# Summing a norm's squares on TensorE, accumulated in PSUM, instead of on GpSimd and VectorE

## The chip, the cores and the metric

The kernel runs on one core of a Trainium2 chip. A core has five engines with queues of their own: TensorE (PE in the profile, its weight loads PEld), VectorE (DVE), ScalarE (ACT), GpSimd (POOL) and SyncE (SP, which here only issues transfers). Matmuls write to PSUM, eight banks per core; VectorE and ScalarE read PSUM, and GpSimd works on SBUF alone in this kernel. The metric is the device time of one execution in microseconds. The time before is the median of three runs.

## What is computed

Two layers of a trunk over 768 tokens (256 context, 512 latent) of width 1024, one sample, all in float32. Each layer has a mixer and a SwiGLU feed-forward (FFN), and ahead of each of the four stands a modulated RMS norm:

```python
def rms_norm(x, gain):
    xf = x.astype(f32)
    y = xf * lax.rsqrt(jnp.mean(xf * xf, axis=-1, keepdims=True) + EPS)
    return (y * gain.astype(f32)).astype(x.dtype)
...
for l in range(DEPTH):
    h = rms_norm(x, norm_mix[l]) * (1.0 + sc_m) + sh_m
    ...                                    # mixer of the layer, added to x
    hf = rms_norm(x, norm_ffn[l]) * (1.0 + sc_f) + sh_f
    x = x + g_f * swiglu(hf, ffn_w_in[l], ffn_w_out[l])
```

The context tokens go the same way with a modulation of their own in layer 0. The norm that changes is the one ahead of layer 1's mixer, whose input is the output of layer 0's FFN.

## The kernel before, in words

Features lie on the partitions: the stream `x` is eight tiles `x[0]` to `x[7]` of 128 features by 768 tokens. Every dense product is done as three matmuls of split operands (`mm3`, L180): weights and activations are each cut into a high part (`whi`, `hhi`) and a rest (`wlo`, `hlo`).

A scheduler at build time orders the instructions of each engine by priority (the order in which the code is written) and by its own model of when operands are ready. What it wrote down is fixed: an engine executes its queue in that order, and an instruction that waits holds up all that stand behind it on the engine. A tile of a pool with so many buffers waits for the release of an older one. In PSUM the pool `gs` has tags A and B with three banks each and C with two; the norms' sums (`sp`) and broadcasts (`rb`) are of tag C.

Layer 0's FFN ends so (`ffn0`, its last group of hidden tiles): for the feature tiles c = 0, 1, 2 the output product is done for all tokens; for c = 3 to 7 it is done token segment by token segment, first the 256 context tokens (segment 0), then tokens 256 to 511 of the tile (segment 1), then 512 to 767 (segment 2). A product of one c and one segment is 12 matmuls (`f<-mid,v`), and VectorE adds it to `x[c]` (L1592). Behind each, the norm of layer 1's mixer (class `Norm`, named `n1m` in the table `NORMS`) takes up what is there:

- `acc(k, i)`: ScalarE squares tile k of segment i into a buffer `sq` of two (L322), and GpSimd adds it to the segment's sum `ssq` (L324), from k = 5 on VectorE does. The first square of a segment is written into `ssq` itself.
- `finish(i)`: a pair of matmuls of `ssq` with a column of ones sums over the partitions, into a PSUM tile `sp` (L335), one column for each 128 tokens. ScalarE scales it to the mean `ms` (L337); a reciprocal root of 128 by 2 numbers follows, its first step on VectorE (L194) and fourteen small steps on GpSimd (L197 to L206); a pair of matmuls with the unit matrix spreads it over the partitions, `rb` (L341). Then VectorE forms `nt` for each k (L344), ScalarE `hhi` (L356) and VectorE `hlo` (L357), the operands of the mixer's first products (`d<-whi,hhi`), which start with segment 1.

The same class serves the norm ahead of layer 0's FFN (`n0f`, three segments, whose end is at 700 to 727 us) and the norm ahead of layer 1's FFN (`n1f`, two segments, at 1551 to 1575 us). There the sums stay as they are.

Of the kernel before, what the change touches and what calls it, by code (L numbers as in the profile page):

```python
# [7 lines left out]
F32 = mybir.dt.float32  # L8
F32R = mybir.dt.float32r
I32 = mybir.dt.int32  # L10
AF = mybir.ActivationFunctionType
# [8 lines left out]
KT = 8  # L20
# [11 lines left out]
RS_SEED = -1.8352575e-20  # L32

ORDER = "vp0 out1 Ad0 Bd1 vp1 Bd2 Bd3 Ad1 Ad2 G2 G0 Ad3 G1 G3".split()
NORMS = dict(n0f=(5, 'G', (7,)), n1m=(5, 'G', (7,)), n1f=(4, 'G', ()))
FILL = dict(out1=2, Ad0=1, vp1=2, Ad2=1, G2=3, Ad3=1, G1=3)

CONST_W = {}
# [88 lines left out]
def build(tc, a, out, dbg=None):  # L127
    nc = tc.nc
    V, G, S, T, DMA = nc.vector, nc.gpsimd, nc.scalar, nc.tensor, nc.sync
    es = ExitStack()  # L130
    with es:
# [10 lines left out]
        def cc(name):  # L142
            o, n = CONST_W[name]
            return cst[:, o:o + n]

        ident, ones = cc("ident"), cc("le")[:, 127:128]
# [156 lines left out]
        class Norm:  # L303
# [11 lines left out]
            def acc(self, k, i):  # L315
                s, sl = self.segs[i]
                n = sl.stop - sl.start
                first = self.ssq[i] is None
                if first:
                    self.ssq[i] = self.tile(f"ssq{i}", n)  # L320
                sq = self.ssq[i] if first else self.tile("sq", 256, 2)
                S.activation(out=sq, in_=self.x[k][:, sl], func=AF.Square)  # L322
                if not first:
                    (V if k >= self.on_v else G).tensor_tensor(out=self.ssq[i], in0=self.ssq[i], in1=sq, op=ALU.add)  # L324

            def finish(self, i):
                s, sl = self.segs[i]
                n = sl.stop - sl.start
                m = n // 128
                if self.h is None:  # L330
                    self.h = new_h()
                hi, lo = self.h
                sp = self.ps.tile([128, 8], F32, name="sp", tag="C")
                for j in range(m):
                    T.matmul(out=sp[:, j:j + 1], lhsT=self.ssq[i][:, 128 * j:128 * j + 128], rhs=ones, start=True, stop=True)  # L335
                ms = self.tile("ms", m)
                S.activation(out=ms, in_=sp[:, 0:m], func=AF.Identity, scale=1.0 / D, bias=epst)  # L337
# [4 lines left out]
                for k in range(KT):  # L342
                    t = self.tile("nt", 256, 4)
                    V.scalar_tensor_tensor(  # L344
                        out=t, in0=self.x[k][:, sl], scalar=self.av[s][:, k:k + 1], in1=rb, op0=ALU.mult, op1=ALU.mult
# [116 lines left out]
        with tc.tile_pool(name="x0", bufs=1) as x0p:  # L462
# [7 lines left out]
            for k in range(KT):  # L470
                sq = ssq if k == 0 else x0p.tile([128, NT], F32, name="sq", tag="sq", bufs=2)
# [4 lines left out]
            for j in range(4):  # L476
# [10 lines left out]
                sp = x0v.tile([128, 6], F32, name="sp", tag="v3")  # L487
# [6 lines left out]
                for i, sl in enumerate((CTX, LAT)):  # L494
                    n = sl.stop - sl.start
# [1478 lines left out]
```

## Time and profile before

| | |
|---|---|
| median of 3 runs | 1938.0 us (1934.97 to 1938.1) |
| the profiled execution, and its span | 1938.09 us, span 1936.3 us |
| TensorE busy | 1794.5 us, 93% of the span |
| VectorE, ScalarE, GpSimd busy | 1257.4, 805.2, 380.5 us |
| sums of squares on GpSimd, in the three norms that use `Norm` (L324) | 30, of 0.73 to 1.55 us |
| the same on VectorE | 26, of 0.42 us |
| squares on ScalarE (L322) | 64, of 0.42 us |

Times below are microseconds from the span's start. In a row of the timeline stand the start, the time that the entry takes, the engine, the line, the operation, output and inputs, and how many instructions were merged; in brackets the idle time of the engine ahead of it and what ended it. A float32 matmul of this kernel that isn't of split operands shows as two weight loads and two matmuls, so that a pair of them (`sp`, `rb`) is "x4".

### The profile page before, as it was taken

To read this page: it belongs to the slowest core of one execution; us is meant where nothing else is said; L and a number is where in the kernel's file an instruction comes from. 1 tells how busy PE (TensorE), PEld (TensorE's weight loads), DVE (VectorE), ACT (ScalarE), POOL (GpSimd) and SP (SyncE) were. 2 spreads that over 40 slices of the span, in tenths; PEclk is the share of its full clock that TensorE was granted. 3 is DMA by queue.
4 is the path that set the end of the run, shared out by engine and by line. 5 is a ranking of instruction groups with operands and counts; after the bars stand their busy time and mean duration, and the time that the engine had idled before them with its cause. 6 is when DMAs were issued, how large, how long until landed. Compare 5 with 4: busy or idle time off the path is not lost.

```text
span 1936.3 us, 30405 instructions
## 1 busy us (share of the span) xinstructions
PE 1794.5 (93%) x11343; PEld 1623.0 (84%) x11343; DVE 1257.4 (65%) x2839; ACT 805.2 (42%) x1773; POOL 380.5 (20%) x436
## 2 busy tenths in 40 slices
PE   4979999788988958999999999899999989999999
PEld 3867889677877857999999999899999778888887
DVE  6566688676767569988877878746666663433333
ACT  3434454446465355232323323455555342222221
POOL 2132214441201052141231322401010020000000
PEclk8989999899999979999999999899999989999999
DMA  7466645656344622424344334212111212323232
GB/s 300 147 192 206 208 128 151 187 158 196 115 122 152 210 83 66 131 98 124 109 138 138 122 122 133 91 45 77 56 62 45 88 45 87 111 78 119 87 105 92
DMA packets 114436, 238.43 MB, mean 123 GB/s; under 512 B 11920, under 2 KB 51088, under 8 KB 113136
## 3 DMA queue, kind: packets, MB, share of 16 engines
q1 hardware_dynamic: 101760, 208.32, 33.8%
q0 software_dynamic: 4064, 14.38, 2.6%
q10 hardware_dynamic: 8464, 13.79, 2.0%
q8 instruction: 90, 1.47, 0.3%
q14 instruction: 58, 0.48, 0.1%
HBM read 203.44 MB, written 32.99 MB: 122 GB/s over the span
## 4 chain that ended last, share of the span: by engine, by line
PE 72%; DVE 6%; DMA 5%; ACT 3%; POOL 2%; issue 2%; SPq 0%; POOLq 0%; ACTq 0%; DVEq 0%
PE f L180 43%; PE d L180 16%; PE o L180 3%; DMA qkd<-ar 1%; PE sc L1779 1%; PE o L1804 1%; PE m L954 1%; PE S L1250 1%; PE t L1278 1%; DMA st<-in_ada_w_dram 1%; PE m L1793 1%; DVE e L1264 0%; PE m L1052 0%; PE m L1750 0%; PE m L1066 0%
## 5 line engine op out<-in xcount | busy, mean ns | idle before, releaser
L166 ACT ACTIVATE whi<-st 128x1024 fp32r<-128x1024 f32 (+6 forms) x191 | 169.6, 889 | 402.7 <-PE f L180 234.3
L167 DVE TENSOR_TENSOR wlo<-st,whi 128x1024 fp32r<-128x1024 f32 (+6 forms) x191 | 195.9, 1027 | 147.7 <-ACT whi L166 145.6
L180 PE MATMUL d<-whi,hhi 128*128 128x256 f32 (+1 forms) x800 | 235.3, 296 | 18.0 <-ACT ar L211 13.6
L180 PE MATMUL d<-wlo,hhi 128*128 128x256 f32 (+1 forms) x800 | 233.2, 292 | 1.3 <-DVE wlo L167 1.3
L180 PE MATMUL d<-whi,hlo 128*128 128x256 f32 (+1 forms) x800 | 232.7, 292 | 0.0
L180 PE MATMUL f<-hlo,whi 128*128 128x512 f32 (+2 forms) x632 | 229.2, 363 | 2.6 <-DVE hlo L400 2.3
L180 PE MATMUL f<-hhi,whi 128*128 128x512 f32 (+2 forms) x632 | 228.5, 363 | 2.6 <-DVE ev L1549 1.3
L180 PE MATMUL f<-hhi,wlo 128*128 128x512 f32 (+2 forms) x632 | 228.2, 362 | 0.3 <-DVE wlo L1520 0.3
L180 PEld LDWEIGHTS d<-whi,hhi 128*128 128x128 f32 x800 | 157.2, 197 | 24.1 <-ACT ar L211 14.9
L180 PEld LDWEIGHTS d<-wlo,hhi 128*128 128x128 f32 x800 | 157.5, 197 | 2.5 <-DVE wlo L167 1.7
L180 PEld LDWEIGHTS d<-whi,hlo 128*128 128x128 f32 x800 | 157.0, 197 | 1.0
L180 PE MATMUL f<-mid,whi 128*128 128x512 f32 (+1 forms) x624 | 151.5, 337 | 0.0
L180 PE MATMUL f<-v,whi 128*128 128x384 f32 x528 | 138.4, 341 | 3.5 <-ACT v L399 2.2
L180 PEld LDWEIGHTS f<-hlo,whi 128*128 128x128 f32 x632 | 119.5, 189 | 16.6 <-DVE hlo L400 2.8
L180 PEld LDWEIGHTS f<-hhi,whi 128*128 128x128 f32 x632 | 119.3, 189 | 16.4 <-ACT hf L383 1.6
L180 PEld LDWEIGHTS f<-hhi,wlo 128*128 128x128 f32 x632 | 119.5, 189 | 13.6 <-DVE wlo L1520 0.5
L180 PEld LDWEIGHTS f<-mid,whi 128*128 128x128 f32 x624 | 106.9, 189 | 12.8
L1477 POOL TENSOR_TENSOR ws<-st 128x512 f32<-128x512 f32 x22 | 33.3, 1511 | 406.0 <-DMA st<-in_wfi_dram 289.9
L180 PE MATMUL d<-hhi,whi 128*128 128x512 f32 (+1 forms) x304 | 107.7, 354 | 2.8 <-ACT cin L211 1.4
L180 PE MATMUL d<-hhi,wlo 128*128 128x512 f32 (+1 forms) x304 | 105.5, 348 | 0.0
L180 PE MATMUL d<-hlo,whi 128*128 128x512 f32 (+1 forms) x304 | 105.4, 347 | 0.0
L180 PE MATMUL f<-mid,wlo 128*128 128x256 f32 (+1 forms) x312 | 102.5, 336 | 0.0
(410 smaller groups left out, 4348.5 us busy)
## 6 DMA issues: line engine op xcount, KB each, us to landing
st<-in_wfi_dram SPq DMA_DIRECT2D x88, 512.0 KB, 3.3
ast<-in_ada_t_dram SPq DMA_DIRECT2D x96, 256.0 KB, 2.9
st<-in_ada_w_dram SPq DMA_DIRECT2D x32, 512.0 KB, 4.0
aw<-in_ada_dram SPq DMA_DIRECT2D x8, 1024.0 KB, 12.5
st<-in_wfo_dram SPq DMA_DIRECT2D x32, 256.0 KB, 2.9
st<-in_w1kv_dram SPq DMA_DIRECT2D x16, 512.0 KB, 3.2
aqT<-qkd SPq DMA_DIRECT2D x48, 128.0 KB, 3.1
st<-in_wfo_dram SPq DMA_DIRECT2D x16, 384.0 KB, 3.0
```

What stands on the lines that cost most here:

```text
L166: S.activation(out=hi, in_=st, func=AF.Copy)
L167: last_lo[:] = [V.tensor_tensor(out=lo, in0=st, in1=hi.bitcast(F32), op=ALU.subtract).ins]
L180: r = T.matmul(out=ps, lhsT=p, rhs=q, start=(c == 0), stop=(c == n - 1))
L954: T.matmul(out=ps[:, i, :], lhsT=lhs[:, c, :], rhs=rhs[:, c, :], start=True, stop=True)
L1250: T.matmul(out=ps[:, o:o + w], lhsT=u.q[:, part, :], rhs=kst[:, m, sl], start=(i == 0), stop=(i == 1))
L1278: T.matmul(out=ov, lhsT=PT[:, i, :], rhs=vt[:, u.kts[i], :], start=(i == 0), stop=(i == u.nk - 1))
L1477: G.tensor_tensor(out=sa[:, 0:512], in0=a21, in1=a22, op=ALU.add)
L1779: T.matmul(out=o, lhsT=lq[:, q], rhs=kv(lk), start=(i == 0), stop=(i == 2))
L1793: T.transpose(out=tp[:, 128 * i:128 * i + 128], in_=E[:, qi, 128 * b:128 * b + 128], identity=ident)
L1804: T.matmul(out=o, lhsT=lv[:, v, :], rhs=p, start=(n == 0 and i == 0), stop=(n == 5 and i == 2))
```

## The change

For the norm `n1m` alone, the sum over feature tiles moves to TensorE: each square, still made on ScalarE, is at once multiplied with the column of ones, and the eight products of a segment accumulate in its two columns of a PSUM tile `sp`, which is now taken from tag C when the segment's first square is there and is held until ScalarE has read the mean. So there are 24 pairs of small matmuls (new line 326) in place of 3 (L335), and 12 additions on GpSimd and 9 on VectorE go. For all norms of the class the buffers `sq` are four and no longer two.

```diff
-NORMS = dict(n0f=(5, 'G', (7,)), n1m=(5, 'G', (7,)), n1f=(4, 'G', ()))
+NORMS = dict(n0f=(5, 'G', (7,)), n1m=(None, 'G', (7,)), n1f=(4, 'G', ()))
...
     def acc(self, k, i):
         s, sl = self.segs[i]
         n = sl.stop - sl.start
         first = self.ssq[i] is None
+        if self.on_v is None:
+            if first:
+                self.ssq[i] = self.ps.tile([128, 512], F32, name="sp", tag="C")
+            sq = self.tile("sq", 256, 4)
+            S.activation(out=sq, in_=self.x[k][:, sl], func=AF.Square)
+            m = n // 128
+            for j in range(m):
+                self.last = T.matmul(
+                    out=self.ssq[i][:, j:j + 1], lhsT=sq[:, 128 * j:128 * j + 128], rhs=ones,
+                    start=(k == 0 and j == 0), stop=(k == KT - 1 and j == m - 1),
+                ).ins
+            return
         if first:
             self.ssq[i] = self.tile(f"ssq{i}", n)
-        sq = self.ssq[i] if first else self.tile("sq", 256, 2)
+        sq = self.ssq[i] if first else self.tile("sq", 256, 4)
...
     def finish(self, i):
-        sp = self.ps.tile([128, 8], F32, name="sp", tag="C")
-        for j in range(m):
+        sp = self.ssq[i] if self.on_v is None else self.ps.tile([128, 8], F32, name="sp", tag="C")
+        for j in range(0 if self.on_v is None else m):
             T.matmul(out=sp[:, j:j + 1], lhsT=self.ssq[i][:, 128 * j:128 * j + 128], rhs=ones, start=True, stop=True)
```

In the changed kernel the lines behind this place are 12 higher (L341 is L353 there, L344 is L356).

How the scheduler orders the engines then is best seen at three places. The first is TensorE where layer 0's FFN ends and layer 1 begins. Before, the end of the last product (`f_13079`), the broadcast of segment 1 (`rb_12975`), the sum of segment 2 (`sp_13096`) and the mixer's first product stand there:

```order
L180 MATMUL f_13079<-mid_11940,v8_12701 128x256 x2
L180 MATMUL f_13079<-mid_11940,v9_12702 128x256
L180 MATMUL f_13079<-mid_11941,v8_12701 128x256 x2
L180 MATMUL f_13079<-mid_11941,v9_12702 128x256
L341 MATMUL rb_12975<-cst_64,rs_y_12957 128x128 [waits Activation_49,Pool_49]
L341 MATMUL rb_12975<-cst_64,rs_y_12957 128x128
L335 MATMUL sp_13096<-cst_64,ssq2_12567 128x1 [waits DVE_49]
L335 MATMUL sp_13096<-cst_64,ssq2_12567 128x1
L180 MATMUL d_13190<-whi_13180,hhi0_12792 128x256 [waits Activation_49]
```

Now thirteen pairs of sums stand between the last product (`f_13102`) and the mixer's first; of them the last pair of segment 1 (`sp_12568`), the last five of segment 2 (`sp_12573`), and the broadcasts of segment 0 (`rb_12848`) and of segment 1 (`rb_12994`):

```order
L326 MATMUL sp_12568<-cst_64,sq_12970 128x1
L326 MATMUL sp_12573<-cst_64,sq_13044 128x1 [waits Activation_49]
L326 MATMUL sp_12573<-cst_64,sq_13044 128x1
L326 MATMUL sp_12573<-cst_64,sq_13062 128x1 [waits Activation_49]
L326 MATMUL sp_12573<-cst_64,sq_13062 128x1
L326 MATMUL sp_12573<-cst_64,sq_13080 128x1 [waits Activation_49]
L326 MATMUL sp_12573<-cst_64,sq_13080 128x1
L353 MATMUL rb_12848<-cst_64,rs_y_12830 128x128 [waits Activation_49,Pool_49]
L353 MATMUL rb_12848<-cst_64,rs_y_12830 128x128
L326 MATMUL sp_12573<-cst_64,sq_13098 128x1 [waits Activation_49]
```

The broadcast of segment 0, which stood among the products of segment 2 before, and the sum of segment 1, which stood there too, are now behind the last product. The other eleven of the 24 pairs, all eight of segment 0 and the first three of segment 1, stand among the products.

The second place is VectorE at the same point of the program. Before, the first step of segment 1's root (`rs_y_12957`) comes ahead of the last two additions to `x`:

```order
L344 SCALAR_TENSOR_TENSOR nt_12834<-x0_7335,gain101_10050,rb_12831 128x256 [waits PE_49]
L344 SCALAR_TENSOR_TENSOR nt_12838<-x1_7336,gain101_10050,rb_12831 128x256
L344 SCALAR_TENSOR_TENSOR nt_12842<-x2_7337,gain101_10050,rb_12831 128x256
L344 SCALAR_TENSOR_TENSOR nt_12846<-x3_7338,gain101_10050,rb_12831 128x256
L324 TENSOR_TENSOR ssq2_12567<-ssq2_12567,sq_13059 128x256 [waits Activation_49,Pool_49]
L194 TENSOR_SCALAR rs_y_12957<-ms_12955 128x2 [waits Activation_49]
L357 SCALAR_TENSOR_TENSOR hlo0_12800<-nt_12834,scal10_8235,hhi0_12792 128x256 [waits Activation_49]
L1592 SCALAR_TENSOR_TENSOR x6_7341<-f_13062,scal02_2663,x6_7341 128x256 [waits PE_49]
```

Now the step of segment 0 (`rs_y_12830`) is just ahead of the last addition to `x`, and that of segment 1 (`rs_y_12976`) stands behind four `nt` of segment 0, which wait for `rb_12848`:

```order
L1604 SCALAR_TENSOR_TENSOR x6_7341<-f_13084,scal02_2663,x6_7341 128x256 [waits PE_49]
L194 TENSOR_SCALAR rs_y_12830<-ms_12828 128x2 [waits Activation_49]
L1604 SCALAR_TENSOR_TENSOR x7_7342<-f_13102,scal02_2663,x7_7342 128x256 [waits PE_49]
L356 SCALAR_TENSOR_TENSOR nt_12851<-x0_7335,gain101_10050,rb_12848 128x256 [waits DVE_49,PE_49]
L356 SCALAR_TENSOR_TENSOR nt_12855<-x1_7336,gain101_10050,rb_12848 128x256 [waits DVE_49]
L356 SCALAR_TENSOR_TENSOR nt_12859<-x2_7337,gain101_10050,rb_12848 128x256 [waits DVE_49]
L356 SCALAR_TENSOR_TENSOR nt_12863<-x3_7338,gain101_10050,rb_12848 128x256 [waits DVE_49]
L194 TENSOR_SCALAR rs_y_12976<-ms_12974 128x2 [waits Activation_49,Pool_49]
```

The whole norm of segment 0 moved from the products of segment 2 to behind them, and the root of segment 1 moved behind it.

The third place is GpSimd in the other norm, `n0f`, where only the number of `sq` buffers changes. Before, the root of segment 0 (`rs_y_7498`, `rs_t_7499`) has four additions of segment 2 (`ssq2_7708`) and two of the next stage's weight sums (`ws`) among its steps:

```order
L205 TENSOR_SCALAR rs_t_7499<-rs_t_7499 128x2 [waits Pool_49]
L324 TENSOR_TENSOR ssq2_7708<-ssq2_7708,sq_7718 128x256 [waits Activation_49]
L206 TENSOR_TENSOR rs_y_7498<-rs_y_7498,rs_t_7499 128x2 [waits Pool_49]
L1477 TENSOR_TENSOR ws_7929<-st_7927 128x512 [waits DMAHW1_49,DVE_49]
L200 TENSOR_TENSOR rs_t_7499<-rs_y_7498 128x2 [waits Pool_49]
L324 TENSOR_TENSOR ssq2_7708<-ssq2_7708,sq_7729 128x256 [waits Activation_49]
L1478 TENSOR_TENSOR ws_7929<-ws_7929,st_7925 128x512 [waits DMAHW0_49,Pool_49]
L201 TENSOR_TENSOR rs_t_7499<-rs_t_7499,rs_v_7500 128x2 [waits Pool_49]
L324 TENSOR_TENSOR ssq2_7708<-ssq2_7708,sq_7740 128x256 [waits Activation_49,Pool_49]
L205 TENSOR_SCALAR rs_t_7499<-rs_t_7499 128x2 [waits Pool_49]
L324 TENSOR_TENSOR ssq2_7708<-ssq2_7708,sq_7751 128x256 [waits Activation_49,Pool_49]
L206 TENSOR_TENSOR rs_y_7498<-rs_y_7498,rs_t_7499 128x2 [waits Pool_49]
```

Now the additions come ahead of the root's chain:

```order
L336 TENSOR_TENSOR ssq2_7708<-ssq2_7708,sq_7718 128x256 [waits Activation_49]
L198 TENSOR_SCALAR rs_v_7500<-ms_7496 128x2 [waits Activation_49]
L336 TENSOR_TENSOR ssq2_7708<-ssq2_7708,sq_7729 128x256 [waits Pool_49]
L336 TENSOR_TENSOR ssq2_7708<-ssq2_7708,sq_7740 128x256 [waits Activation_49,Pool_49]
L197 TENSOR_SCALAR rs_y_7498<-rs_y_7498 128x2 [waits DVE_49]
L336 TENSOR_TENSOR ssq2_7708<-ssq2_7708,sq_7751 128x256 [waits Activation_49,Pool_49]
L200 TENSOR_TENSOR rs_t_7499<-rs_y_7498 128x2 [waits Pool_49]
L201 TENSOR_TENSOR rs_t_7499<-rs_t_7499,rs_v_7500 128x2 [waits Pool_49]
```

Four additions have left the middle of this chain; the two weight sums are still in it. SyncE's transfers are the same and in the same order in both kernels.

## The prediction

> **What bounds the kernel now.** I read the page's busy shares and its chain first, then TensorE's waits around the norm, then the timeline of each engine there.
>
> ```profile
> PE 1794.5 (93%) x11343; PEld 1623.0 (84%) x11343; DVE 1257.4 (65%) x2839; ACT 805.2 (42%) x1773; POOL 380.5 (20%) x436
> PE 72%; DVE 6%; DMA 5%; ACT 3%; POOL 2%; issue 2%; SPq 0%; POOLq 0%; ACTq 0%; DVEq 0%
> ```
>
> TensorE is busy for 93% of the span and makes 72% of the chain that ended last. So work that is put on TensorE's queue lengthens the run unless it falls into a hole there, and work taken from GpSimd (20% busy) or VectorE helps only where TensorE waits for it. This is TensorE's timeline from the FFN's last segment products to the mixer's first product:
>
> ```profile
> 1221.72 12.75 PE L180 MATMUL f<-mid,v 128*128 128x256 f32 x105
> 1234.31 0.50 PE L335 MATMUL sp<-cst,ssq 128*128 128x1 f32 x4
> 1234.67 6.83 PE L180 MATMUL f<-mid,v 128*128 128x256 f32 x55
> 1241.34 0.60 PE L341 MATMUL rb<-cst,rs_y 128*128 128x128 f32 x4
> 1241.78 0.50 PE L335 MATMUL sp<-cst,ssq 128*128 128x1 f32 x4
> 1242.14 2.63 PE L180 MATMUL f<-mid,v 128*128 128x256 f32 x20
> 1249.54 1.22 PE L341 MATMUL rb<-cst,rs_y 128*128 128x128 f32 x4 [4.77 <-POOL rs_y L206]
> 1250.56 0.85 PE L335 MATMUL sp<-cst,ssq 128*128 128x1 f32 x4
> 1252.22 0.58 PE L180 MATMUL d<-whi,hhi 128*128 128x256 f32 x1 [0.81 <-ACT hhi L356]
> ```
>
> The 180 products run without a gap, 0.120 us each (12.59 us for 105). A pair of `sp` takes 0.36 us of the stream (1234.31 to 1234.67, 1241.78 to 1242.14), an `rb` pair 0.44. The last product ends at 1244.77; TensorE then waits 4.77 us for the root of segment 1, and the mixer's first product starts at 1252.22. That hole of 7.45 us is all that the change can win or lose here: segment 0's norm was hidden under segment 2's products, segment 1's sum too.
>
> **The change on TensorE's stream.** By the instruction order eleven of the 24 pairs stand among the products, and two `sp` pairs and segment 0's `rb` leave them: 11 x 0.36 - 2 x 0.36 - 0.44 = +2.8 us. Nothing hides this, since the stream has no gap there. The last product ends at 1247.57, and the queue is free for the rest at 1221.72 + 180 x 0.12 + 11 x 0.36 = 1247.28. The Trainium skill (TensorE: Matmul & The Clock Gate, LDWEIGHTS) lets a weight load cost its 128 columns over 1.2 GHz, 107 ns, however few columns are then streamed; by that the eleven pairs, of four loads each, would take 4.7 us rather than 3.96, an estimate by that page, and the row's 0.36 us decides.
>
> Do squares hold up the eleven? Of the four `sq` buffers segment 2's first three squares occupy three until its PSUM tile is free, which is after segment 0's mean is read; so one buffer goes round among the other squares. One round is a square, a pair and two signals, about 0.42 + 0.36 + 0.5; the pairs of k = 3 to 7 of segment 0 stand 23 products apart, 2.8 us. I cost that at nothing: the products cover it. The price if the cover fails is a rival.
>
> **The change behind the last product.** Here the order puts, one behind the other: three pairs of segment 2, five of segment 1, three of segment 2, `rb` of segment 0, two pairs, `rb` of segment 1. The last five squares of segment 1 had no buffer before. These rows price the steps:
>
> ```profile
> 1234.99 0.24 ACT L337 ACTIVATE ms<-sp,epst 128x2 f32<-128x2 f32 x1
> 1222.06 1.02 ACT L322 ACTIVATE ssq<-x 128x256 f32<-128x256 f32 x3
> 1251.51 0.26 ACT L337 ACTIVATE ms<-sp,epst 128x2 f32<-128x2 f32 x1 [2.11 <-PE sp L335]
> 1251.67 1.70 ACT L356 ACTIVATE hhi<-nt,scal 128x256 fp32r<-128x256 f32 x4
> 1241.98 1.66 DVE L344 SCALAR_TENSOR_TENSOR nt<-x,gain,rb 128x256 f32<-128x256 f32 x4 [0.44 <-PE rb L341]
> 1250.80 1.26 DVE L344 SCALAR_TENSOR_TENSOR nt<-x,gain,rb 128x256 f32<-128x256 f32 x3 [0.97 <-PE rb L341]
> 1251.98 0.16 DVE L194 TENSOR_SCALAR rs_y<-ms 128x2 int32<-128x2 int32 x1
> 1252.30 0.22 POOL L197 TENSOR_SCALAR rs_y<-rs_y 128x2 f32<-128x2 f32 x1 [0.22 <-DVE rs_y L194]
> 1244.21 0.30 POOL L197 TENSOR_SCALAR rs_y<-rs_y 128x2 f32<-128x2 f32 x1 [1.31 <-DVE rs_y L194]
> 1249.20 0.29 POOL L206 TENSOR_TENSOR rs_y<-rs_y,rs_t 128x2 f32<-128x2 f32 x1
> 713.61 0.22 POOL L197 TENSOR_SCALAR rs_y<-rs_y 128x2 f32<-128x2 f32 x1 [0.80 <-DVE rs_y L194]
> 717.04 0.20 POOL L206 TENSOR_TENSOR rs_y<-rs_y,rs_t 128x2 f32<-128x2 f32 x1
> ```
>
> 1. Segment 0's last pair stands 13 products ahead of the end: it starts at 1247.28 - 1.56 - 0.36 = 1245.36 and ends 0.50 later, its mean comes 0.18 behind and takes 0.24 (as at 1234.81 to 1235.23), so 1246.28. GpSimd's part of the root starts some 0.5 later, 1246.8.
> 2. That part lasted 5.33 us (1244.21 to the broadcast at 1249.54) with VectorE busy beside it, and 3.63 to 3.7 in the other norm (713.61 to 717.24). Here VectorE has little to do, so 3.7: segment 0's root is ready at 1250.5.
> 3. The eleven pairs behind the last product: ScalarE can make a square each 0.30 us (three in 1.02), TensorE needs 0.36 for a pair, so 11 x 0.36 = 3.96, done at 1251.24. This is later than the root, so `rb` of segment 0 starts then if the clock holds.
> 4. The clock may fall on the way:
>
> ```profile
> 1247.00:1248.00 1.00, 0.00 (x0) 0.00 (x0) 1.00 (x4) 0.78 (x3) 0.84 (x3) 0.82 1.00 375
> 704.00:705.00 1.00, 0.00 (x0) 0.00 (x0) 0.00 (x0) 0.23 (x1) 1.00 (x4) 0.96 0.00 0
> 1250.00:1255.00 5.00, 4.19 (x21) 4.11 (x21) 4.20 (x12) 2.44 (x7) 2.76 (x10) 0.50 0.01 2
> ```
>
> These are windows of TensorE, its loads, VectorE, ScalarE, GpSimd, then the granted clock. It went from 1.00 to 0.50 at 1247.64, 2.9 us after the last product (0.82 is the mean of that microsecond), and stood at 0.50 later, where the `sp` pair took 0.85 in place of 0.50 and `rb` 1.22 in place of 0.60. Whether one-column matmuls keep the clock up no row shows. Between 3.96 us and twice that I take 4.5, since most of the eleven run before the fall: `rb` of segment 0 at 1251.8.
> 5. From `rb` to the first `nt` 1.26 us (1249.54 to 1250.80), four `nt` 1.57, then VectorE's step of segment 1's root at 1254.6 and GpSimd's part 0.3 behind (1251.98 to 1252.30), 1254.9. VectorE is full with segment 0's `nt` and `hlo` meanwhile, so I take the 5.33: `rb` of segment 1 at 1260.2, against 1249.54. That is +10.7. VectorE is done with segment 0 in time: from 1253.1 fifteen operations of 0.39, to 1259.0.
> 6. Behind it segment 2's mean no longer stands ahead of the first `hhi` on ScalarE (it held it from about 1251.35 to 1251.67): -0.3. The first product starts 10.4 us later than before; the mixer's order from there is the same, and TensorE's queue carries the delay on.
>
> The 12 additions on GpSimd and 9 on VectorE that go are worth nothing of their own: they lay beside the products, and what waited for the last of them now waits for TensorE's own queue.
>
> **The other two norms.** With four `sq` buffers, `n0f` changes on GpSimd:
>
> ```profile
> 710.07 1.22 PE L341 MATMUL rb<-cst,rs_y 128*128 128x128 f32 x4 [9.37 <-POOL rs_y L206]
> 695.79 2.45 POOL L324 TENSOR_TENSOR ssq<-ssq,sq 128x256 f32<-128x256 f32 x3 [1.72 <-ACT sq L322]
> 700.35 0.24 POOL L198 TENSOR_SCALAR rs_v<-ms 128x2 f32<-128x2 f32 x1
> 704.00 0.73 POOL L324 TENSOR_TENSOR ssq<-ssq,sq 128x256 f32<-128x256 f32 x1
> ```
>
> TensorE waits 9.37 us there for a root that GpSimd started at 700.35 and in which four additions of 0.73 lie. They leave it, and GpSimd's wait of 1.72 us for a square, which two buffers caused, makes room for them ahead of it. At best all four are won, 2.9 us; at worst the root starts as much later, 0. One of them still stands between the root's first steps and it starts a little later: I take -1.8. `n1f` keeps its order on TensorE and GpSimd; 0.
>
> **Sum.** 10.4 - 1.8 = +8.6 us on the profiled execution's 1938.09 (span 1936.3 and 1.8 around it), 1946.7; the median lies 0.1 lower, so 1946.5. About 0.2%, 3.9 us, is what a measurement of this kernel can tell from no change.
>
> **Bounds.** Low: GpSimd's root at 3.7 (-1.6), the clock stays up (-1.1, half of it in `rb`), 2.9 in `n0f` (-1.1): 1942.7. High: all eleven pairs at twice 0.36 (+3.4) and nothing in `n0f` (+1.8): 1951.7. The Trainium skill (GPSIMD Engine Reference, Specifications) says that GpSimd shares its SBUF interfaces with VectorE and suffers from VectorE's operations with two SBUF inputs; `hlo` is one, so by that rule the 5.33 of step 5 is the right end, and 5.33 beside 3.7 agrees with it.
>
> **Rivals.**
> - The sums run at the half clock. For it: the fall came 2.9 us after the last product, and one column streams little. Against it: the fall must come early in a stretch of 4 us. +3.4 us, 1950. 0.15. The Trainium skill (TensorE: Matmul & The Clock Gate, Part 1) has the clock halve after an idle window of about 3.4 us that runs free; by that rule, if such matmuls count as idle, the fall lies at the end of the stretch, which is the forecast; the trace's 2.9 agrees.
> - Squares come late and TensorE waits inside the products. For it: one buffer goes round. Against it: 2.8 us of room for 1.3 us. If it fails for the five pairs of k = 3 to 7 by half a microsecond each, +2.5: 1949. 0.08.
> - Not slower: the relieved VectorE and GpSimd shorten segment 1's root and its sum still comes before the products' end. Then the 1.31 us for VectorE's step (1244.21) and 1.6 of the root go from the wait of 4.77, and 2.8 - 2.9 - 1.8 = -1.9: 1936. It decides at whether segment 1's last pair runs more than two products before the end. The written order, which TensorE keeps, speaks against it. 0.05.
> - The delay is half absorbed, because segment 1's root starts early or `n0f` gains 3: 1942. 0.07.
>
> The forecast has 0.65. Slower than 1941.9 takes the first two rivals and half of the last with it: 0.89; no change 0.09; faster 0.02. The range 1942.5 to 1951 leaves out the third rival, part of the last and the far end of the first.
>
> **What would show it.** Right: `sp` pairs of 0.36 us among the products, no wait of TensorE for a square there, and the last product 2.8 us later; then 11 pairs in 4 to 5 us; a wait of TensorE for GpSimd's `rs_y` ahead of the second `rb`, of some 6 to 7 us; the first `rb` of `n0f` at about 708. Wrong: waits for ScalarE's `sq` among the products, a root of segment 1 that is not behind segment 0's `nt`, a mixer whose end moves by less than its first product.

## The result and the profile after

| | before | after |
|---|---|---|
| median | 1938.1 us (1934.97 to 1946.66, 5 runs) | 1954.1 us (1946.68 to 1958.48, 5 runs) |
| ratio to before | | 1.0080 (1.0056 to 1.0104) |
| span of the profiled execution | 1936.3 us | 1955.1 us |

The changed kernel is 0.8% slower, some 15.5 us (10.9 to 20.2). A ratio here and below is to runs of before that were taken beside those of the kernel; the brackets hold its 95% interval. The forecast was 1946.5 with a range to 1951: the direction is right, the loss is nearly twice as large. TensorE's share and the chain of the page after:

```profile
PE 1807.2 (92%) x11427; PEld 1634.1 (84%) x11427; DVE 1254.5 (64%) x2830; ACT 803.4 (41%) x1773; POOL 368.7 (19%) x424
PE 72%; DVE 9%; DMA 8%; ACT 4%; issue 3%; POOL 3%; SPq 0%; ACTq 0%; POOLq 0%; DVEq 0%
```

TensorE has 84 more matmul records, VectorE and GpSimd the 9 and 12 fewer additions. This is TensorE's timeline from the first of the segment products to the mixer's first product (the sums are L326, `rb` is L353):

```profile
1228.45 2.19 PE L180 MATMUL f<-mid,v 128*128 128x256 f32 x17
1230.49 0.95 PE L326 MATMUL sp<-cst,sq 128*128 128x1 f32 x8
...
1237.23 2.99 PE L180 MATMUL f<-mid,v 128*128 128x256 f32 x23
1240.05 0.50 PE L326 MATMUL sp<-cst,sq 128*128 128x1 f32 x4
...
1253.16 1.79 PE L180 MATMUL f<-mid,v 128*128 128x256 f32 x13
1254.79 5.88 PE L326 MATMUL sp<-cst,sq 128*128 128x1 f32 x44
1260.53 1.20 PE L353 MATMUL rb<-cst,rs_y 128*128 128x128 f32 x4
1261.52 1.71 PE L326 MATMUL sp<-cst,sq 128*128 128x1 f32 x8
1268.86 1.22 PE L353 MATMUL rb<-cst,rs_y 128*128 128x128 f32 x4 [5.63 <-POOL rs_y L206]
1271.20 0.58 PE L180 MATMUL d<-whi,hhi 128*128 128x256 f32 x1 [1.11 <-ACT hhi L368]
```

The stretch takes 42.75 us, 30.50 before: +12.25 where 10.4 was forecast. No sum among the products has a wait in brackets. The wait ahead of the second `rb` is 5.63 us, and what it waits for started late; here VectorE and GpSimd ahead of it:

```profile
1261.77 1.66 DVE L356 SCALAR_TENSOR_TENSOR nt<-x,gain,rb 128x256 f32<-128x256 f32 x4 [6.30 <-PE rb L353]
1263.34 0.16 DVE L194 TENSOR_SCALAR rs_y<-ms 128x2 int32<-128x2 int32 x1
1263.66 0.30 POOL L197 TENSOR_SCALAR rs_y<-rs_y 128x2 f32<-128x2 f32 x1 [4.59 <-DVE rs_y L194]
```

Segment 1's root starts behind segment 0's four `nt`, as forecast; GpSimd had stood idle for 4.59 us.

The rest of the difference lies elsewhere. Both kernels were profiled again below (before twice in all, after three times), so each stage can be set beside its own scatter. Stages are bounded by the first product of each kind on TensorE: `o` (the end of layer 0's mixer), `f<-v` (layer 0's FFN), `f<-mid,v` (the segment products), `d<-whi,hhi` (layer 1's mixer).

| stage, us | before | after | difference of means |
|---|---|---|---|
| start to first `o` | 681.45, 680.40 | 685.85, 686.78, 683.35 | +4.4 |
| `o` to FFN (holds `n0f`) | 39.92, 40.10 | 40.79, 40.17, 40.34 | +0.4 |
| FFN to segment products | 500.35, 500.70 | 501.81, 501.93, 501.03 | +1.1 |
| segment products to mixer (holds `n1m`) | 30.50, 30.50 | 42.75, 42.34, 43.58 | +12.4 |
| mixer to end | 684.08, 683.50 | 683.90, 683.78, 685.60 | +0.6 |
| span | 1936.3, 1935.2 | 1955.1, 1955.0, 1953.9 | +18.9 |

The stage of the changed norm repeats within 1.3 us; the mixer of layer 0, ahead of the change, scatters by 1 to 3.

### The profile page after: what moved, and what is told of

Read it like the earlier page. It is cut to its first block, busy times and chain, and to the rows that moved or that the text cites. A ratio compares the mean times of both kernels' runs of the same rounds, so it can differ in the third digit from the quotient of the medians.

```text
span 1955.1 us, 30550 instructions
## 1 busy us (share of the span) xinstructions
PE 1807.2 (92%) x11427; PEld 1634.1 (84%) x11427; DVE 1254.5 (64%) x2830; ACT 803.4 (41%) x1773; POOL 368.7 (19%) x424
## 3 DMA queue, kind: packets, MB, share of 16 engines
q1 hardware_dynamic: 101760, 208.32, 33.7%
## 4 chain that ended last, share of the span: by engine, by line
PE 72%; DVE 9%; DMA 8%; ACT 4%; issue 3%; POOL 3%; SPq 0%; ACTq 0%; POOLq 0%; DVEq 0%
PE f L180 43%; PE d L180 15%; DMA qkd<-ar 2%; PE o L180 2%; DVE cv L463 1%; PE vp L560 1%; DMA st<-in_ada_w_dram 1%; PE sc L1791 1%; PE o L1816 1%; DMA qkvd<-cv 1%; PE S L1262 1%; PE m L1805 1%; PE m L966 1%; PE t L1290 1%; PE sp L326 0%
## 5 line engine op out<-in xcount | busy, mean ns | idle before, releaser
L180 PE MATMUL d<-whi,hhi 128*128 128x256 f32 (+1 forms) x800 | 235.5, 296 | 19.3 <-ACT ar L211 13.6
L180 PEld LDWEIGHTS f<-hhi,wlo 128*128 128x128 f32 x632 | 120.2, 190 | 13.6 <-DVE wlo L1532 0.5
L180 PEld LDWEIGHTS f<-v,whi 128*128 128x128 f32 x528 | 98.0, 193 | 5.9 <-ACT v L411 2.5
```

What stands on the lines that cost most here:

```text
L180: r = T.matmul(out=ps, lhsT=p, rhs=q, start=(c == 0), stop=(c == n - 1))
```

## The experiments

The theory after the result: the change costs so much because three early squares of segment 2 hold three of the four `sq` buffers and wait for a PSUM bank, so that most sums and segment 0's `rb` fall behind the last product. The rival: 24 pairs on TensorE cost 24 times their price wherever they stand. The other questions were what a pair costs, what `n0f`'s two more buffers do, and what is only scatter.

### Four buffers alone

```diff
-                sq = self.ssq[i] if first else self.tile("sq", 256, 2)
+                sq = self.ssq[i] if first else self.tile("sq", 256, 4)
```

> The kernel before with four sq buffers instead of two for all its norms; layer 1's sums stay additions. It takes the n0f part of the change alone. Theory A (the prediction's step): GpSimd's additions of later segments move ahead of segment 0's root, TensorE's first wait for rs_y in n0f falls from 9.37 us towards 7, and the run is 1.8 us faster, 1936. Theory B (read from the profile after, where that wait was 11.6 us): with more buffers more additions stand on GpSimd inside the root, the wait is 11 to 12 us, and the run is 2 to 3 us slower, 1940 to 1941. Theory C: the 6.7 us by which the profile after is late when the last products of layer 0's FFN start is variation between executions of layer 0's mixer: then this kernel's products of n0f's o start within some us of 681.45 either way, and its median is within 2 us of 1938.

1941.85 against 1939.24, ratio 1.0008 (0.9995 to 1.0022): theory A's gain of 1.8 us (0.9991) lies outside the interval, and the time does not tell theory B from theory C. TensorE's wait is theory B's. First before's second profile, then this kernel's rows on TensorE and GpSimd:

```profile
709.20 1.22 PE L341 MATMUL rb<-cst,rs_y 128*128 128x128 f32 x4 [9.37 <-POOL rs_y L206]
```

```profile
711.56 1.22 PE L341 MATMUL rb<-cst,rs_y 128*128 128x128 f32 x4 [11.50 <-POOL rs_y L206]
```

```profile
695.35 3.32 POOL L324 TENSOR_TENSOR ssq<-ssq,sq 128x256 f32<-128x256 f32 x4 [0.53 <-ACT sq L322]
699.96 1.98 POOL L324 TENSOR_TENSOR ssq<-ssq,sq 128x256 f32<-128x256 f32 x1 [1.29 <-ACT sq L322]
701.91 0.24 POOL L198 TENSOR_SCALAR rs_v<-ms 128x2 f32<-128x2 f32 x1
702.13 1.52 POOL L324 TENSOR_TENSOR ssq<-ssq,sq 128x256 f32<-128x256 f32 x2
703.73 1.07 POOL L197 TENSOR_SCALAR rs_y<-rs_y 128x2 f32<-128x2 f32 x1
704.76 0.72 POOL L324 TENSOR_TENSOR ssq<-ssq,sq 128x256 f32<-128x256 f32 x1
```

One more addition went ahead of the root, and GpSimd waits 1.29 us for its square; three of the four others did not leave the root but moved to its first steps. The root starts at 701.91, 1.9 us behind the end of the last `o` product (700.06); before, it started at 700.35, 0.4 us ahead of it. Not all of the longer wait is the buffers': the `o` products took 19.25 and 19.43 us in the two profiles of before, where the granted clock was 0.83 on average from 680 to 690 us, and 17.93 us here at 1.00, so TensorE began to wait sooner. From the first `o` product to this `rb` it is 29.43 us here, 28.62 and 28.80 in before.

### Segment 2's early squares

Four kernels call fewer of them early. With none early ("late"), the loop over the first three feature tiles leaves segment 2 out and its three squares come behind segment 1's norm:

```diff
-                    for q in range(3):
+                    for q in range(2):
                         nn.acc(c, q)
...
                 for q, sg in enumerate(fine):
+                    for c in range(KT - tail if q == 2 else 0):
+                        nn.acc(c, q)
                     for c in cs:
```

> The kernel after, with segment 2's first three squares (and their sums) called behind segment 1's norm instead of in the loop over the first three feature tiles. Nothing holds three of the four sq buffers then, and segment 2 asks for its PSUM bank only behind segment 0's and 1's rb. The order then has 16 pairs of segments 0 and 1 and segment 0's rb among the products, segment 1's rb right behind the last one, segment 2's eight pairs after it. Theory 1 (held buffers and banks make the delay): 16 pairs x 0.43 - 2 x 0.36 = +6.2 us in the stream, TensorE's wait ahead of segment 1's rb falls from 5.63 (4.77 before) to about 2.2, so from the start of the products to the first mixer product 35 us (30.5 before, 42.75 after), and the run is some 7 us faster than after and 5 to 7 slower than before, 1943 to 1945. Theory 2 (24 pairs on TensorE's queue cost 24 x 0.43 = 10.3 wherever they stand): that stretch is 41 to 43 us as in after, and the run 1951 or more.

1947.91 against 1939.24, ratio 1.0046 (1.0029 to 1.0062); 36.6 us for the stretch (1222.43 to 1259.03). Segment 1's `rb` and what follows:

```profile
1254.38 0.71 PE L353 MATMUL rb<-cst,rs_y 128*128 128x128 f32 x4 [1.26 <-POOL rs_y L206]
1254.93 4.24 PE L326 MATMUL sp<-cst,sq 128*128 128x1 f32 x24
1259.03 0.56 PE L180 MATMUL d<-whi,hhi 128*128 128x256 f32 x1
```

The same 24 pairs, two of them now among the mixer's first products, and 6 us less in the stretch, some 7 by the ratios: the rival, with its 41 us or more, falls. Theory 1 holds, though the stretch is 1.6 us over its 35 and the run 3 us over its window. With one early (`range(3 if c < 1 else 2)`), the bank is held as in after but one buffer only:

> The kernel after, but of segment 2's first three squares only that of feature tile 0 is called in the early loop, the other two behind segment 1's norm. Segment 2's PSUM tile is still asked for behind segment 0's and ahead of the rb's, so its bank is held as in after and segment 1's rb still stands behind all 24 pairs; but one sq buffer is held in place of three. It separates held buffers from held banks. If the buffers made the delay: segment 0's rb is back among the products, three pairs stand behind the last product, and from the products' start to the first mixer product it takes 21.6 + 21 x 0.43 + 0.44 + 3 x 0.5 + 0.5 + 2.34 = 35.4 us (42.75 in after, 36.6 with late squares); the run 1943 to 1946. If the bank alone makes segment 1's rb late, the stretch stays above 40 us and the run above 1950.

1947.37 against 1936.93, ratio 1.0050 (1.0030 to 1.0070); 37.2 us, 1.8 over what was expected of the buffers and 3 under what was expected of the bank. Segment 0's `rb` stands among the products again, segment 1's behind all 24 pairs, where 1.36 us for segment 2's last square and 0.91 for the root are waited for:

```profile
1248.51 0.61 PE L353 MATMUL rb<-cst,rs_y 128*128 128x128 f32 x4
...
1254.99 0.60 PE L326 MATMUL sp<-cst,sq 128*128 128x1 f32 x4 [1.36 <-ACT sq L323]
1256.50 0.71 PE L353 MATMUL rb<-cst,rs_y 128*128 128x128 f32 x4 [0.91 <-POOL rs_y L206]
```

So the held buffers are the larger part: with two of the three free again, 5.6 of after's 42.75 us are gone, or some 4 of the 41.3 that after takes where the clock stays up during the sums (64 columns, below). The held bank and the one buffer left cost up to 3.5 us: with none early and the clock up (64 columns again) the stretch takes 33.7, and some 0.9 of that difference are the two pairs among the mixer's products. With two early (`c < 2`):

> The kernel after, with segment 2's squares of feature tiles 0 and 1 called early and that of tile 2 late: two of the four sq buffers are held, between the kernel with one (37.2 us from the products' start to the first mixer product, 1947.4) and the kernel after with three (42.3 to 43.6 us, 1954 to 1955). By the held buffers: segment 0's rb still stands among the products, 10 + 15 products ahead of their end, 21 of 24 pairs too, so 35.4 to 37.5 us and 1944 to 1948. If three are not needed for the delay and the order of the early squares alone makes it, 40 us or more. Its first o product tells of the open part: with 4.4 us more ahead of it in the three profiles of the changed kernel (683.35 to 686.78) than in both of before, and 677.99 to 682.13 in all kernels that call segment 2's squares late, this kernel should be at 683 or more if the early squares go with it, at 678 to 682 if chance or something else does.

1946.53 against 1938.21, ratio 1.0043 (1.0027 to 1.0060), inside the window for two held buffers. The profiled execution, at 1955.45 the slowest of its nine, has 40.8 us in the stretch, of which 3.4 were lost to a fall of the clock shown at the end; the remaining 37.4 are near the 37.2 with one. The step is at three held of four.

A bank of the products' group A for segment 2's sums lets its squares go on early:

```diff
-                        self.ssq[i] = self.ps.tile([128, 512], F32, name="sp", tag="C")
+                        self.ssq[i] = self.ps.tile([128, 512], F32, name="sp", tag="CCA"[i])
```

> The kernel after with segment 2's sums in a bank of the products' A group instead of the C group; four sq buffers, squares as early as in after. It takes away what holds segment 2's first squares (the bank that segment 0's sum gives back) and what makes rb of segments 0 and 1 wait for banks. Theory 1 (held banks, and the sq buffers held through them): segment 0's rb stands among the products again; from the products' start to the first mixer product 21.6 + 24 x 0.42 + 0.44 + 2.8 = 35 us as with late squares (36.6 there), and the run is 1944 to 1948 against 1954 for after. Theory 2 (only the sq buffers' number counts; banks don't matter): 42 us as in after. If one bank less in group A holds the products up, gaps appear among them and the gain is eaten.

1948.56 against 1938.34, ratio 1.0046 (1.0026 to 1.0066), half a microsecond above theory 1's window. Its order mixes earlier products into the stretch, so the way from the first FFN product to the mixer is compared: 539.5 us, 538.1 with late squares, 544.6 in after, 530.9 before. And segment 2 by additions as before, only segments 0 and 1 by matmuls (`self.on_v is None and i < 2`):

> The kernel after, but segment 2's squares are added on GpSimd and VectorE as before; segments 0 and 1 are summed by matmuls. No third PSUM tile is asked for while two hold open sums, and segment 2's squares go one by one into its running sum. Theory 1 (the held buffers and bank): sixteen pairs and segment 0's rb stand among the products, segment 1's rb behind the last one with a wait of about 1.3 us as with late squares; from the products' start to the first mixer product 21.6 + 16 x 0.43 + 0.44 + 0.36 + 1.3 + 2.7 = 33.3 us; with n0f's part (+1) the run is at 1942 to 1943, +0.2%. Theory 2 (the sums on TensorE cost the delay by themselves, sixteen of 24 pairs): two thirds of after's loss, 38.7 us in that stretch, 1948 to 1949.

1944.55 against 1939.84, ratio 1.0032 (1.0018 to 1.0046); 34.7 us in the stretch, 1.4 over theory 1 and 4.0 under theory 2. Segment 1's `rb` waits 3.05 us, not 1.3:

```profile
1246.25 5.38 PE L180 MATMUL f<-mid,v 128*128 128x256 f32 x43
1254.68 1.10 PE L353 MATMUL rb<-cst,rs_y 128*128 128x128 f32 x4 [3.05 <-POOL rs_y L206]
```

### What a pair costs

The kernel with late squares, with `sq` written as fp32r and two columns of fp32r ones, so that a pair has two loads, not four:

```diff
-                    sq = self.tile("sq", 256, 4)
+                    sq = self.pool.tile([128, 256], F32, name="sq", tag="sq", bufs=4).bitcast(F32R)
...
-                            out=self.ssq[i][:, j:j + 1], lhsT=sq[...], rhs=ones,
+                            out=self.ssq[i][:, 2 * j:2 * j + 2], lhsT=sq[...], rhs=self.ones,
```

> As the kernel with segment 2's squares called late, and the squares written as fp32r with two columns of fp32r ones, so that a pair of sums is two loads and two matmuls instead of four and four. If the loads set a pair's price (0.43 us by four), a pair is about 0.2 us: 16 pairs add 3.4 us to the stream, segment 1's sum ends 39 products before the end and its rb waits about 2.5 us; the stretch from the products' start to the first mixer product is 31 to 32 us (30.5 before) and the run within 2 us of the kernel before with four buffers. If a pair's price is a fixed cost per matmul that fp32r doesn't halve (0.4), the stretch stays at 35 and the run at 1943 to 1945.

1940.4 against 1939.24, ratio 1.0009 (0.9995 to 1.0022).

```profile
1224.61 0.50 PE L329 MATMUL sp<-onr,sq 128*128 128x2 f32 x4
1226.01 0.28 PE L329 MATMUL sp<-onr,sq 128*128 128x2 f32 x2
1249.25 0.71 PE L356 MATMUL rb<-cst,rs_y 128*128 128x128 f32 x4 [1.06 <-POOL rs_y L206]
1252.36 0.40 PE L180 MATMUL d<-whi,hhi 128*128 128x256 f32 x1
```

From 1222.58 to 1248.19, where the wait for `rb` begins: 25.61 us, less 180 x 0.12 and 0.44 for the other `rb`, is 3.57 for 16 pairs, 0.22 each. So the price goes by the number of loads and matmul passes, which fp32r halves together. The stretch takes 29.8 us, 0.7 less than before.

Two further steps on this kernel: 128 equal columns instead of two, and then two `sq` buffers for the other norms, with layer 1's squares in the three tiles of `n0f`'s running sums.

> As the kernel with late squares of segment 2 and fp32r sums, but each sum streams 128 equal columns of ones instead of two. In that kernel the eight pairs behind segment 1's rb ran while the granted clock fell (0.80 at 1252, 0.50 from 1253 to 1255), and the mixer's first products took 0.21 us each instead of 0.12. If columns streamed keep the clock up (as 64 fp32 columns did), the clock stays at 1.00 from segment 1's rb on, some 20 products of the mixer are 0.09 us shorter, 1.5 to 2.5 us in all, and the run is at 1938 to 1939 against 1940.4 for two columns and 1939.2 for before. If one fp32r pass of 128 columns still counts as little, the clock falls as it did and the time is the same 1940 to 1941. If 128 columns cost more than the load hides, each of 16 pairs in the stream is dearer than 0.22 us and the run 1 us or more slower.

> As the kernel with late squares, fp32r sums and 128 columns, and the other norms have their two sq buffers back: layer 1's squares go round the three tiles that n0f used for its running sums. It separates n0f's part. If four buffers made n0f late, TensorE's first wait for rs_y is 9.4 us again (11.5 to 11.6 in every kernel with four buffers), the way from the o products to the first product of the FFN is 39.9 us instead of 40.8, and the run is 0.9 us faster than with four, about 1937.5. Three buffers instead of four for layer 1's squares may hold segment 2's sums, of which the order puts two pairs into the mixer's first products: at most +1. If the 9.37 of the profile before was only one execution's, the wait stays above 11.

128 columns: 1940.53 against 1938.34, ratio 1.0011 (0.9994 to 1.0029), no gain; the clock fell to 0.50 at 1253 all the same, behind a pause of some 2 us for segment 1's root. With two buffers: 1938.5, ratio 0.9998 (0.9981 to 1.0014), and `n0f`'s wait is 9.70 us:

```profile
705.62 1.22 PE L357 MATMUL rb<-cst,rs_y 128*128 128x128 f32 x4 [9.70 <-POOL rs_y L206]
```

From `o` to the FFN it takes 38.93 to 40.10 us in the three profiles with two buffers (mean 39.65), 40.02 to 42.14 in all thirteen with four (mean 41.0). So four buffers cost `n0f` about 1.3 us, though the three profiles of after alone give 0.4. This last kernel is level with before; none is measurably faster than it.

### One column and the clock

The kernel after, with 64 columns of ones in each sum (the mean reads one of them):

```diff
-                            out=self.ssq[i][:, j:j + 1], lhsT=sq[...], rhs=ones,
+                            out=self.ssq[i][:, 64 * j:64 * j + 64], lhsT=sq[...], rhs=ones.to_broadcast([128, 64]),
```

> The kernel after with 64 columns of ones instead of one in each sum (64 equal columns of sums, of which the mean reads one); order as in after. It asks whether the clock falls during the eleven pairs behind the last product because one column streams so little. Theory 1 (few columns count as idle): with 64 columns the granted clock stays at 1.00 through the pairs, from the last product (1254.7 in after) to the wait ahead of segment 1's rb; the eleven pairs take 11 x 0.4 = 4.4 us in place of 5.7, segment 0's rb 0.5 instead of 1.2; the first mixer product 2 to 3 us earlier, 1951 to 1952. Theory 2 (the clock falls by a clock of its own, some 3 to 4 us after the products end, whatever stands there): the same 0.81 and 0.50 in the fifth microsecond, the same 5.7 us, no change of time against after. If 64 columns cost more than the load hides, the pairs in the stream go from 0.43 to 0.6 or more and the run is 2 us or more slower than after.

Windows of after (TensorE's busy time, its loads, VectorE, ScalarE, GpSimd, then the granted clock and two figures on DMA), then of this kernel, both behind the last product:

```profile
1256.00:1258.00 2.00, 2.00 (x20) 2.00 (x19) 0.00 (x0) 1.83 (x5) 1.39 (x7) 1.00 0.73 222
1258.00:1260.00 2.00, 2.00 (x14) 2.00 (x13) 0.00 (x0) 1.40 (x5) 0.22 (x1) 0.65 0.11 41
1260.00:1262.00 2.00, 2.00 (x11) 2.00 (x11) 0.23 (x1) 0.00 (x0) 0.00 (x0) 0.50 0.00 0
```

```profile
1258.00:1260.00 2.00, 2.00 (x20) 2.00 (x20) 0.00 (x0) 1.83 (x5) 1.36 (x7) 1.00 0.81 251
1260.00:1262.00 2.00, 2.00 (x20) 2.00 (x20) 0.16 (x1) 0.89 (x4) 0.22 (x1) 1.00 0.00 0
```

TensorE is busy throughout in both, yet with one column the clock goes to 0.50, 3.8 us into the sums, and with 64 it stays (it falls later, at 1264.03, in the wait for segment 1's root). The eleven pairs took 4.86 us (1256.28 to 1261.14) against 5.74, the stretch 41.3 against 42.75. The time, 1951.71 against 1939.24, ratio 1.0063 (1.0042 to 1.0084), does not separate it from after.

The same fall stands inside the products of the kernel with late squares, where TensorE has no gap at all:

```profile
1226.00:1228.00 2.00, 2.00 (x19) 2.00 (x20) 0.84 (x2) 1.01 (x2) 0.00 (x0) 1.00 0.86 246
1228.00:1230.00 2.00, 2.00 (x13) 2.00 (x13) 1.23 (x1) 0.77 (x2) 0.00 (x0) 0.65 0.40 164
1230.00:1232.00 2.00, 2.00 (x12) 2.00 (x11) 0.48 (x1) 0.42 (x1) 0.00 (x0) 0.50 0.58 176
1232.00:1234.00 2.00, 2.00 (x19) 2.00 (x19) 0.48 (x1) 0.00 (x0) 0.00 (x0) 1.00 0.21 86
```

At half clock for 2 x 0.70 + 2.0 = 3.4 us, behind six pairs that stood among 11 products within 4 us. So that kernel got 64 columns too:

> The kernel with segment 2's squares called late, with 64 columns of ones in each fp32 sum instead of one. In the one-column kernel the granted clock fell to 0.50 for about 3.4 us while TensorE was busy without a gap (1228.7 to 1232.0, behind six pairs among 19 products), which cost 1.7 us, and again behind the last product (0.97 in 1254 to 1256, then 0.50), where six pairs and the mixer's first products then ran at half clock. If one column counts as idle for the clock and 64 do not, neither fall is there: the 180 products and 16 pairs take 28.9 to 29.5 us to segment 1's rb (30.7 with one column), the first mixer product comes 34 us after the products' start (36.6), its products take 0.12 us from the start, and the run is 3 to 5 us faster than 1947.9, at 1943 to 1945. If the falls are chance, they are there again, and the time is 1946 to 1949.

1944.8 against 1938.21, ratio 1.0037 (1.0020 to 1.0055), which overlaps that with one column; the profiles tell the two apart. Both falls are gone, the stretch takes 33.7 us (1222.12 to 1255.78) instead of 36.6:

```profile
1228.00:1230.00 2.00, 2.00 (x20) 2.00 (x19) 1.62 (x2) 0.62 (x2) 0.00 (x0) 1.00 0.36 143
1230.00:1232.00 2.00, 2.00 (x20) 2.00 (x19) 0.41 (x1) 0.42 (x1) 0.00 (x0) 1.00 0.64 176
...
1254.00:1256.00 2.00, 2.00 (x20) 2.00 (x20) 1.75 (x5) 1.97 (x7) 0.00 (x0) 1.00 0.26 93
```

### The scatter of layer 0's mixer

> The kernel before once more, for a second profile: how much of the profile's differences is variation between executions. If layer 0's mixer varies, the first o product starts some us off 681.45 (680.16 to 686.03 in the kernels with the same order ahead of it); n0f's first wait should be 9 to 10 us if two buffers make it so, and the way from the products' start to the first mixer product 30.3 to 30.7 us.

> The changed kernel once more. Its first profile was 6.7 us late when the last products of layer 0's FFN started, of which 4.4 stood at the first o product (685.85, where six kernels with the same order ahead of it gave 678 to 686). If that is variation between executions, this profile's first o product lies anywhere from 678 to 686, and what is the change's own repeats: n0f's first wait 11.5 us (9.37 in both profiles of before), the way from the first FFN product to the first mixer product 544 to 545 us (530.85 and 531.20 in before), which makes 13.5 to 14.5 us in all, 1951 to 1953 beside 1938. If the change itself makes layer 0's mixer late, the first o product is at 685 or later again and the median at 1954 or more.

> The changed kernel a third time, for its profile only. In two of its profiles (and in the one with 64 columns) the first o product of layer 0's mixer stood at 685.85, 686.78 and 686.03, and in eight profiles of kernels with the same order ahead of it at 678 to 682. Chance would put it near 681 this time; if the change itself makes the mixer late, at 684 or more again.

Before again: 1937.04 us, first `o` at 680.40, `n0f`'s wait 9.37 once more, the stretch 30.50. After again: 1955.3 against 1939.84, ratio 1.0088 (1.0070 to 1.0106), first `o` at 686.78, `n0f`'s wait 10.95, the stretch 42.34. After a third time: 1955.71, first `o` at 683.35, the stretch 43.58; its `n0f` waited only 9.64 us, because its `o` products took longer (19.41 us). The order of all engines ahead of `n0f` is the same in all kernels of this study, but for one ScalarE copy more, of the ones, in the three kernels with fp32r. Still the first `o` stands at 683.35 to 686.78 in the six profiles of after, of 64 columns in after, of the bank of group A and of two early squares, and at 677.99 to 682.19 in the ten others. The medians don't follow: the kernel with two early squares had 686.33 in an execution 9 us above its own median, and the median of 64 columns in after, 1951.7, is what its later stages alone give (10.8 us in the stretch and some 2 elsewhere, on 1939.2). So the lateness belongs to single executions; why it fell on these six profiles stays open.

## Why the prediction was right and wrong

The mechanism of the largest term was right. The time left the range because three terms of the sum were wrong, `n0f` (in sign), the eleven pairs behind the last product and the price of a pair (in size), and because of 1 to 3 us that stay open.

- **Segment 1's root behind four `nt` (step 5, the largest term).** Forecast 8.4 us from `rb` to `rb`, measured 8.33 (1260.53 to 1268.86). Right, and so is step 3's order: segment 0's root was done at 1257.89, ahead of the last of the eleven pairs. Step 6 is right too: `rb` to the first product 2.34 us, 0.34 less than before.
- **Price of a pair in the stream: mis-sized.** 26.34 us from 1228.45 to 1254.79, less 180 x 0.12, is 4.74 for eleven pairs, 0.43 each and not 0.36: +0.8. The row of before showed where the product behind a pair starts, not that the pair itself starts some 0.06 us late behind the last product (23 products from 1237.23 take 2.76, the pair starts at 2.82). The 4.7 us by the Trainium skill (TensorE: Matmul & The Clock Gate, LDWEIGHTS), four loads of 107 ns, which the prediction set aside, agrees with the trace, as does the halving with two loads.
- **The eleven pairs behind the last product (steps 3 and 4): mis-sized.** 5.74 us instead of 4.5. Eleven at 0.43 make 4.7, and 4.86 was measured where the clock stayed up; the other 0.9 is the clock. The second `rb` and the mixer's first product inherit both: 40.41 and 42.75 us behind the products' start, where 38.5 and 40.9 were forecast.
- **`n0f`: wrong in sign.** The forecast let the root start later at worst by as much as it gained, "0". Nothing excluded a loss. It also counted one addition between the root's first steps, where the order shown ahead of it has three behind `rs_v`. The order put one addition more ahead of the root, with a wait for its square, and left three others inside it: about +1.3 by all profiles with four buffers, where -1.8 was forecast.
- **Cover of the squares.** No wait of TensorE for a square among the products; the rival of late squares is excluded. What the buffers did instead was decided when the instructions were ordered: with three of four held, the order itself spaces the pairs 23 products apart and puts 13 pairs and segment 0's `rb` behind the end. The prediction described the hold, but asked only whether the squares come in time; that the hold itself makes about half of the stretch's loss, late squares show: 6 of 12.25 us less, with 22 of the 24 pairs still in it.
- **The other rivals.** That the sums run at half clock came true in part: the clock fell in the middle of them, 3.8, 4.3 and 2.9 us from their start in the three profiles of after, and the eleven pairs took 5.74, 5.34 and 6.58 us. That the 2.9 us of before agree with an idle window of 3.4 us was read too kindly: they are shorter, so that the products' last half microsecond lay in that window. "Not slower" and "half absorbed" did not occur: segment 1's last pair is behind the last product, and nothing of the delay was taken back in the mixer.
- **The sum.** By the profiles the norm's stretch is +12.4 against +10.4, and the two stages around `n0f` together +1.5 against -1.8; these and +0.6 behind make 14.5 us, 1952.6 from 1938.1. The measured medians ratio, 15.5 us (10.9 to 20.2) and 17.1 (13.6 to 20.6), leaves 1 to 3 us that may belong to layer 0's mixer, where no instruction moved, and that the runs do not settle. Of the 5.9 us between 8.6 and 14.5, `n0f`'s two stages are 3.3 and the norm's stretch 2.0. The range held no cost for a stage that the change does not touch, nor for a loss in `n0f`. The chances do not add up either: the forecast, the first two rivals and half of the last make 0.915, not 0.89.

## What to carry to other kernels

An accumulation that stays open in PSUM holds its bank, and the inputs that wait for the bank hold their buffers: count, for each instruction called early, what it keeps from those that are needed first. Small matmuls on a full TensorE queue cost their loads and the gap around them (a pair 0.43 us with four loads, 0.22 with two), so price one from start to start over a stretch that has many, and halve the loads where the precision allows. Give a moved or re-buffered side path a bound on both sides, even where the change seems only to relieve it.

## What was not expected of the hardware

TensorE's clock fell while TensorE was busy without a gap. There it fell only where one-column fp32 matmuls were dense: during the sums behind the products in all three profiles of after; for 3.4 us in the kernel with late squares and in that with a bank of group A (0.55 and 0.59 of two windows of 2 us from 1238 on); and for 6.8 us with two early squares:

```profile
1250.00:1252.00 2.00, 2.00 (x18) 2.00 (x18) 0.43 (x1) 0.72 (x2) 0.00 (x0) 0.97 0.00 0
1252.00:1254.00 2.00, 2.00 (x11) 2.00 (x11) 0.49 (x1) 0.42 (x1) 0.00 (x0) 0.50 0.00 0
1254.00:1256.00 2.00, 2.00 (x11) 2.00 (x11) 0.00 (x0) 0.26 (x1) 0.22 (x1) 0.50 0.00 0
1256.00:1258.00 2.00, 2.00 (x11) 2.00 (x11) 0.49 (x1) 0.42 (x1) 0.00 (x0) 0.50 0.00 0
1258.00:1260.00 2.00, 2.00 (x16) 2.00 (x16) 0.11 (x1) 0.00 (x0) 0.00 (x0) 0.83 0.00 0
```

(2 x 0.03 + 6 + 2 x 0.34 = 6.7 us.) It did not fall there with 64 columns, in either kernel, though the 180 products and eleven pairs took the same (26.33 us from 1229.95 to 1256.28, 26.34 in after). With one early square, where pairs are nearly as dense for a while, it did not fall either. What decides is how much of one step the sums fill: in each of the sixteen profiles the changes of the clock lie whole multiples of 3.41 us apart (late squares: down at 1228.58, up at 1232.00, down at 1255.89). Among the steps through which TensorE was busy at clock 1.00, a fall followed each that held 2.11 us or more of one-column sums (2.11 with two early squares, 2.13 with late ones, 2.23 with the bank of group A, 2.91 to 3.41 in after) and none that held less, of which the fullest had 2.04 (one early, 1243.89 to 1247.30). With 64 columns no fall followed steps with 2.20 us of sums (late squares, 1224.34 to 1227.75) and with nothing but sums (in after, 1257.20 to 1260.61). The Trainium skill (TensorE: Matmul & The Clock Gate, Part 1) has the gate watch a free-running window of about 3.4 us of activity; falls of 3.4 and 6.7 us, one and two such windows, agree with it. Widening a narrow fp32 sum from 1 to 64 columns cost nothing that these profiles show and kept the clock.
